# Sums of weight quarters in a Strassen-like FFN: added by transfers into the buffer instead of by VectorE

## The chip, the core and the metric

The kernel runs on one core of a Trainium2 chip. The metric is the device time of one execution in microseconds, taken without the profiler; the kernel before has a median of 1122.21 us over 3 runs (1121.78 to 1122.27). The engines of the core are TensorE (PE; its weight loads are listed as PEld), VectorE (DVE), ScalarE (ACT), GpSimd (POOL) and SyncE (SP). SP and POOL issue transfers here; 16 DMA queues carry them.

## What is computed

A bidirectional encoder block on 512 tokens of width 1024, in float32: FFN 1, a mixer (a recurrent branch and a neighbourhood attention), FFN 2. Only the two FFNs matter here:

```python
D_MODEL = 1024; SEQ = 512; D_FF = 2816; FFN_RES = 0.5

def _swiglu(h, w_gu, w_down):
    g, u = jnp.split(h @ w_gu, 2, axis=-1)
    return (jax.nn.silu(g) * u) @ w_down

x = x + FFN_RES * _swiglu(_rmsnorm(x, norm_ffn1[l]), w_ffn1_gu[l], w_ffn1_down[l])
...
x = x + FFN_RES * _swiglu(_rmsnorm(x, norm_ffn2[l]), w_ffn2_gu[l], w_ffn2_down[l])
```

## The kernel before

Tokens lie along the free dimension, features along the 128 partitions. To get float32 accuracy out of a faster format, each operand is split in two halves, H (a rounded copy, made by ScalarE, L138) and L (what is left, made by VectorE, L141), and each product takes three matmuls: H with H, H with L, L with H. Such a split of a 128x1024 block of weights is what `operand` does; its results lie in the pools wh and wl, four buffers each.

The hidden dimension has 22 blocks of 128 features. In FFN 1 the first 4 of them, in FFN 2 the first 2, are computed plainly from chunks of w1gu and w2gu. The others go two at a time through `strassen`: 9 units in FFN 1, 10 in FFN 2. A unit computes g and u of two blocks for all tokens. Its weights, as a 2 by 2 matrix (rows: g and u; columns: the two halves of the 1024 inputs) are four quarters of 128x1024 (512 KB) in w1s or w2s, numbered 0 to 3; the tokens are two halves of 256. Instead of eight products of a quarter with a half it makes seven, four of them with sums of quarters and of input tiles (Strassen's method in Winograd's form). Each product is 24 matmuls of 128x128 by 256 tokens and named by its input: a11 takes quarter 0, a12 quarter 2, s4 quarter 3, s1 the sum 0+1, s2 0+1+3, s3 1+3, and a22 0+1+3+2.

Per unit the buffers are a_ (quarter 0, then its running sum), b_ (quarter 3, then 3+1), d (quarter 1) and c (quarter 2). a_ and b_ come from the pool wraw (3 buffers, `load_w` also loads the plain and down-projection weights there), d and c from the pool pair (4 buffers). SP loads all four (L322). The sums are VectorE instructions (L325), each between two splits of the same buffer, run by the helper `after_sum` ahead of their turn (`high_priority`). The last product, a22, of a unit is made in the next unit, between s1 and s2, so TensorE's order within a unit is a11, a12, s1, a22 of the unit before, s2, s4, s3. In the last unit of an FFN, a12 moves behind s3. Results leave PSUM through p1, p5 and u2 (ScalarE L342, L348, L353; VectorE L337, L355, L357), are multiplied by rstd (L303), go through silu (L304) and are multiplied with u (L310).

A scheduler turns the program into one queue per engine, in which instructions run in order, each behind its semaphore waits. Instructions in `high_priority` are moved ahead.

Of the kernel before, what the change touches and what calls it, by code (L numbers as in the profile page):

```python
# [11 lines left out]
AF = mybir.ActivationFunctionType  # L12
ALU = mybir.AluOpType
# [71 lines left out]
def block_kernel(ctx: ExitStack, tc, a, out):  # L85
    nc = tc.nc
# [14 lines left out]
    def nm(s):  # L101
        uid[0] += 1
        return f"{s}_{uid[0]}"
# [3 lines left out]
    def big_t(dt=F32, shape=(P, T), n="b"):  # L107
        return big.tile(list(shape), dt, tag="big", bufs=NBIG, name=nm(n))

    def pair_t():  # L110
        return big.tile([P, 2, T], F32, tag="pair", bufs=4, name=nm("pair"))

    def acc_t():
        return acc.tile([P, T], F32, tag="acc", name=nm("acc"))

    def aux_t():
        return aux.tile([P, T], F32, tag="aux", name=nm("aux"))
# [18 lines left out]
    def split(raw, H, L, act=True):  # L136
        if act:
            nc.scalar.activation(H, raw, AF.Copy)  # L138
        else:
            nc.vector.tensor_copy(H, raw)  # L140
        nc.vector.tensor_tensor(L, raw, H.bitcast(F32), ALU.subtract)  # L141
# [3 lines left out]
    def raw_t():  # L145
        return wpool.tile([P, 1024], F32, tag="wraw", bufs=3, name=nm("wraw"))

    def hl_t():
        return (wpool.tile([P, 1024], F32R, tag="wh", bufs=4, name=nm("wh")),
                wpool.tile([P, 1024], F32R, tag="wl", bufs=4, name=nm("wl")))  # L150
# [124 lines left out]
    def strassen(src, units, A, r, hs, ahead):  # L275

        half = T // 2
        prev = {}
        view = lambda t: t.rearrange("p (m t) -> p m t", m=2)

        def product(ps, w, form, first, last):
            H, L = w
            for m in range(2):
                o = ps[:, m * half : (m + 1) * half]
                for k in range(4):
                    c = slice((m * 4 + k) * P, (m * 4 + k + 1) * P)
                    xh_, xl_ = A[form][k]


                    for w_, x_ in ((H, xh_), (H, xl_), (L, xh_)):  # L290
                        nc.tensor.matmul(o, w_[:, c], x_, start=first and m + k == 0 and w_ is H and x_ is xh_,  # L291
                                         stop=m + k == 4 and w_ is L, skip_group_check=True)

        def operand(raw):
            w = hl_t()
            with tc.high_priority():
                split(raw, *w)
            return w

        def gate(t, tok):  # L300
            rr = r[:, tok].unsqueeze(1).to_broadcast([P, 2, half])
            s_ = big_t(n="s")
            nc.vector.tensor_tensor(view(s_), view(t), rr, ALU.mult)  # L303
            nc.scalar.activation(s_, s_, AF.Silu)  # L304
            return s_

        def put(u, s_, t, tok):
            for m in range(2):
                c = slice(m * half, (m + 1) * half)
                mark["h"] = nc.vector.tensor_tensor(hs[u * 2 + m][:, tok], s_[:, c], t[:, c], ALU.mult)  # L310

        def last_product(p):
            product(p["Z"], p["w"](), "a22", False, True)
            put(p["u"], gate(p["Z"], slice(half, T)), p["u7"], slice(half, T))

        for u in range(units):
            a_, b_ = raw_t(), raw_t()
            d = pair_t().rearrange("p a b -> p (a b)")
            c = pair_t().rearrange("p a b -> p (a b)")

            for t, i in ((a_, 0), (d, 1), (b_, 3), (c, 2)):
                nc.sync.dma_start(t, src[u, i])  # L322

            def add(t, o, i):
                nc.vector.tensor_tensor(t, t, o, ALU.add)  # L325
            def after_sum(t, o, i, add=add):
                with tc.high_priority():
                    add(t, o, i)
                return operand(t)

            Z, X, Y = acc_t(), acc_t(), aux_t()
            hs += [big_t(n="h") for _ in range(2)]
            last = u == units - 1

            def gate1():
                product(Y, w_c, "a12", True, True)
                nc.vector.tensor_tensor(p1, p1, Y, ALU.add)  # L337
                return gate(p1, slice(0, half))

            product(Z, operand(a_), "a11", True, False)  # L340
            p1 = big_t(n="p1")
            nc.scalar.activation(p1, Z, AF.Copy)  # L342
            w_c = operand(c)
            if not last:
                s1 = gate1()
            product(X, after_sum(a_, d, 1), "s1", True, False)
            p5 = big_t(n="p5")
            nc.scalar.activation(p5, X, AF.Copy)  # L348
            if prev:
                last_product(prev)  # L350
            product(Z, after_sum(a_, b_, 3), "s2", False, False)
            u2 = big_t(n="u2")
            nc.scalar.activation(u2, Z, AF.Copy)  # L353
            product(X, operand(b_), "s4", False, True)
            nc.vector.tensor_tensor(u2, u2, X, ALU.add)  # L355
            product(Z, after_sum(b_, d, 1), "s3", False, False)
            nc.vector.tensor_tensor(p5, p5, Z, ALU.add)  # L357
            if last:
                ahead()
                s1 = gate1()  # L360
            put(len(hs) // 2 - 1, s1, u2, slice(0, half))
            prev = dict(u=len(hs) // 2 - 1, Z=Z, u7=p5, w=lambda a_=a_, c=c, f=after_sum: f(a_, c, 2))
        last_product(prev)

    def ffn(wgu, ws, wd, xh, xl, S, ssum, plain, res, emit_out, lead=None, end=None):
# [74 lines left out]
        def ahead(n):  # L440
            while len(cuts) < min(n, len(order)):
                qk = order[len(cuts)]
                cuts[qk] = big_t(F32R, n="hh"), big_t(F32R, n="hl")
                split(hs[qk[1]], *cuts[qk])

        strassen(ws, (FT - plain) // 2, A, r, hs, lambda: ahead(AHEAD))
        for q in range(2):
            outs = range(q * 4, q * 4 + 4)
# [517 lines left out]
    for w, fn, scale in ((0, AF.Gelu_apprx_tanh, 1.0), (1, AF.Tanh, 0.5)):  # L966
        for fs in (range(0, 4), range(4, 8)):
            for f, t in gates(w, fs, fn, scale):
                until("lru", lambda: A[f] is not None)
                if w == 0:  # L970
                    o = big_t(n="A")
# [118 lines left out]
```

## Time and profile before

| | |
|---|---|
| median of 3 runs | 1122.21 us |
| profiled execution, own time | 1122.16 us |
| its span (first to last instruction) | 1119.9 us |
| PE granted clock | 1.0 throughout |
| units of FFN 1 and FFN 2 | 9 and 10, of 20.16 us each |
| product (24 matmuls) | 2.88 us |
| sums on VectorE (L325) | 76, of 1.22 us |
| transfers | 138.04 MB, mean 123 GB/s |

The profile is one execution recorded by the hardware. A line such as "L141 DVE TENSOR_TENSOR wl<-wraw,wh" names the line of the kernel, the engine, the operation and its output and inputs by their tiles, with buffer numbers left out. In a timeline the columns are start (us), duration (us), engine, line, operation, and in brackets the idle time of the engine just before and what ended it. SPq and POOL rows with DMA are the issue of a transfer; the time to its landing is listed apart.

### The profile page before, as it was taken

How to read it: one execution, taken by the hardware profiler on the slowest of the kernel's cores; microseconds unless marked ns; L12 is line 12 of the kernel's file. 1: busy time of each engine (PE TensorE's matmuls, PEld its weight loads, DVE VectorE, ACT ScalarE, POOL GpSimd, SP SyncE). 2: the span in 40 equal slices, each digit the busy share in tenths (PEclk: the TensorE clock that was granted, in tenths of full speed). 3: DMA queues.
4: the chain of work that ended last, by engine and by line, in shares of the span. 5: the costliest groups of instructions: out<-in, count | busy, mean ns of one | idle time of the engine just before them, and what ended most of it. 6: DMA issues, size and time to landing. Idle time of an engine off the chain costs nothing.

```text
span 1119.9 us, 17423 instructions
## 1 busy us (share of the span) xinstructions
PE 1113.1 (99%) x6867; PEld 983.9 (88%) x6867; DVE 835.1 (75%) x1294; ACT 593.0 (53%) x897; POOL 52.4 (5%) x116
## 2 busy tenths in 40 slices
PE   9999999999999999999999999999999999999998
PEld 8899999988888778787888888888999999998887
DVE  7888888894745776998655976659788888894552
ACT  8554554563533669876464564446445455464330
POOL 0000000000000341310110000000000000000000
PEclk9999999999999999999999999999999999999999
DMA  7232333343433585653443332264134233353421
GB/s 265 95 124 85 113 114 95 120 144 95 136 91 107 160 255 154 184 164 95 144 140 104 104 104 72 75 237 164 57 96 131 77 115 113 94 170 95 132 76 38
DMA packets 46770, 138.04 MB, mean 123 GB/s; under 512 B 7008, under 2 KB 10592, under 8 KB 46688
## 3 DMA queue, kind: packets, MB, share of 16 engines
q1 hardware_dynamic: 39744, 118.31, 33.9%
q0 software_dynamic: 6368, 18.36, 5.8%
q8 instruction: 54, 0.88, 0.3%
q10 hardware_dynamic: 576, 0.26, 0.1%
q14 instruction: 28, 0.23, 0.1%
HBM read 120.12 MB, written 8.39 MB: 115 GB/s over the span
## 4 chain that ended last, share of the span: by engine, by line
PE 99%; DVE 0%; ACT 0%; issue 0%; ACTq 0%; DVEq 0%
PE acc L291 29%; PE acc L165 11%; PE acc L166 11%; PE acc L167 11%; PE aux L291 5%; PE acc L763 4%; PE acc L765 4%; PE acc L764 4%; PE aux L165 4%; PE aux L166 4%; PE aux L167 4%; PE aux L898 1%; PE aux L886 1%; PE aux L677 1%; PE aux L857 1%; PE acc L404 1%
## 5 line engine op out<-in xcount | busy, mean ns | idle before, releaser
L138 ACT ACTIVATE wh<-wraw 128x1024 fp32r<-128x1024 f32 (+3 forms) x242 | 239.7, 993 | 304.3 <-PE acc L291 95.9
L141 DVE TENSOR_TENSOR wl<-wraw,wh 128x1024 fp32r<-128x1024 f32 (+3 forms) x254 | 289.1, 1143 | 135.7 <-ACT wh L138 134.7
L291 PE MATMUL acc<-s,wh 128*128 128x256 f32 x1216 | 220.5, 283 | 0.0
L291 PEld LDWEIGHTS acc<-s,wh 128*128 128x128 f32 x1216 | 189.7, 192 | 0.0
L291 PE MATMUL acc<-s,wl 128*128 128x256 f32 x608 | 172.1, 283 | 0.0
L165 PE MATMUL acc<-xh,wh 128*128 128x512 f32 x304 | 121.1, 399 | 0.0
L167 PE MATMUL acc<-xh,wl 128*128 128x512 f32 x304 | 119.0, 391 | 0.0
L166 PE MATMUL acc<-xl,wh 128*128 128x512 f32 x304 | 118.9, 391 | 0.0
L291 PEld LDWEIGHTS acc<-s,wl 128*128 128x128 f32 x608 | 116.7, 192 | 0.0
L291 PE MATMUL acc<-xh,wl 128*128 128x256 f32 x304 | 86.0, 283 | 0.0
L291 PE MATMUL acc<-xl,wh 128*128 128x256 f32 x304 | 86.0, 283 | 0.0
L291 PE MATMUL acc<-xh,wh 128*128 128x256 f32 x304 | 86.0, 283 | 0.0
L763 PE MATMUL acc<-wh,xh 128*128 128x512 f32 x192 | 75.6, 394 | 0.0
L765 PE MATMUL acc<-wl,xh 128*128 128x512 f32 x192 | 74.9, 390 | 0.0
L764 PE MATMUL acc<-wh,xl 128*128 128x512 f32 x192 | 74.9, 390 | 0.0
L325 DVE TENSOR_TENSOR wraw<-wraw,pair 128x1024 f32<-128x1024 f32 x57 | 69.6, 1220 | 0.8
L165 PE MATMUL aux<-hh,wh 128*128 128x512 f32 (+1 forms) x181 | 69.9, 386 | 0.0
L166 PE MATMUL aux<-hl,wh 128*128 128x512 f32 (+1 forms) x181 | 69.9, 386 | 0.0
L167 PE MATMUL aux<-hh,wl 128*128 128x512 f32 (+1 forms) x181 | 69.9, 386 | 0.0
L165 PEld LDWEIGHTS acc<-xh,wh 128*128 128x128 f32 x304 | 57.1, 188 | 12.8 <-issue 1.7
L167 PE MATMUL acc<-hh,wl 128*128 128x512 f32 (+1 forms) x176 | 67.9, 386 | 0.0
L166 PE MATMUL acc<-hl,wh 128*128 128x512 f32 (+1 forms) x176 | 67.9, 386 | 0.0
(212 smaller groups left out, 2215.6 us busy)
## 6 DMA issues: line engine op xcount, KB each, us to landing
wraw<-wqkv SPq DMA_DIRECT2D x24, 512.0 KB, 4.8
wraw<-wg SPq DMA_DIRECT2D x24, 512.0 KB, 3.6
wraw<-w1d SPq DMA_DIRECT2D x22, 512.0 KB, 3.6
wraw<-w2d SPq DMA_DIRECT2D x22, 512.0 KB, 3.6
pair<-w2s SPq DMA_DIRECT2D x20, 512.0 KB, 3.6
wraw<-w2s SPq DMA_DIRECT2D x20, 512.0 KB, 3.7
wraw<-w1s SPq DMA_DIRECT2D x18, 512.0 KB, 3.6
pair<-w1s SPq DMA_DIRECT2D x18, 512.0 KB, 3.6
```

Of the source, the lines that this page charges most:

```text
L138: nc.scalar.activation(H, raw, AF.Copy)
L141: nc.vector.tensor_tensor(L, raw, H.bitcast(F32), ALU.subtract)
L165: nc.tensor.matmul(ps, wh, xh, start=first, stop=False, skip_group_check=skip)
L166: nc.tensor.matmul(ps, wh, xl, start=False, stop=False, skip_group_check=skip)
L167: mark["mm"] = nc.tensor.matmul(ps, wl, xh, start=False, stop=last, skip_group_check=skip)
L291: nc.tensor.matmul(o, w_[:, c], x_, start=first and m + k == 0 and w_ is H and x_ is xh_, stop=m + k == 4 and w_ is L, skip_group_check=True)
L325: nc.vector.tensor_tensor(t, t, o, ALU.add)
L404: nc.tensor.matmul(pre[i], w[i][1][:, s], xh[k], start=k == 0, stop=False)
L677: prev, mm = mm, nc.tensor.matmul(ps[d][b], W[w][o, c], X[x][o], start=x == 1, stop=w + x == 0)
L763: nc.tensor.matmul(pss[j], xh[kk][:, tj], H[:, s], start=kk == 0, stop=False)
L764: nc.tensor.matmul(pss[j], xl[kk][:, tj], H[:, s], start=False, stop=False)
L765: mark["mm"] = nc.tensor.matmul(pss[j], xh[kk][:, tj], L[:, s], start=False, stop=kk == KT - 1)
```

## The change

The sums move from VectorE to the transfers: a quarter is loaded by a GpSimd transfer that adds what it brings to what is in the buffer (`accum_op=ALU.add`). There are four such per unit: quarters 1, 3 and 2 into a_, one after the other, each behind the split of the sum before it, and quarter 3 into d, which holds quarter 1; s3 then reads d. b_ and c are only read. The 76 VectorE sums are gone. Each unit now moves eight quarters instead of four, four by SP and four by GpSimd. The load of a_, its product a11 and the copy into p1 stand in a function `begin`, called at the head of a unit (`begun` stays empty).

```diff
+        def begin(u):
+            a_ = raw_t()
+            nc.sync.dma_start(a_, src[u, 0])
+            Z = acc_t()
+            product(Z, operand(a_), "a11", True, False)
+            p1 = big_t(n="p1")
+            nc.scalar.activation(p1, Z, AF.Copy)
+            return a_, Z, p1
+
+        def add(u, t, i):
+            with tc.high_priority():
+                nc.gpsimd.dma_start(t, src[u, i], accum_op=ALU.add)
+
+        begun = {}
         for u in range(units):
-            a_, b_ = raw_t(), raw_t()
+            a_, Z, p1 = begun.pop(u) if u in begun else begin(u)
+            b_ = raw_t()
             d = pair_t().rearrange("p a b -> p (a b)")
             c = pair_t().rearrange("p a b -> p (a b)")
-            for t, i in ((a_, 0), (d, 1), (b_, 3), (c, 2)):
+            add(u, a_, 1)
+            for t, i in ((c, 2), (d, 1), (b_, 3)):
                 nc.sync.dma_start(t, src[u, i])
-            def add(t, o, i):
-                nc.vector.tensor_tensor(t, t, o, ALU.add)
-            def after_sum(t, o, i, add=add):
-                with tc.high_priority():
-                    add(t, o, i)
-                return operand(t)
+            add(u, d, 3)
...
-            product(X, after_sum(a_, d, 1), "s1", True, False)
+            w = operand(a_)
+            add(u, a_, 3)
+            product(X, w, "s1", True, False)
...
-            product(Z, after_sum(a_, b_, 3), "s2", False, False)
+            w = operand(a_)
+            add(u, a_, 2)
+            product(Z, w, "s2", False, False)
...
-            product(Z, after_sum(b_, d, 1), "s3", False, False)
+            product(Z, operand(d), "s3", False, False)
...
-            prev = dict(u=len(hs) // 2 - 1, Z=Z, u7=p5, w=lambda a_=a_, c=c, f=after_sum: f(a_, c, 2))
+            prev = dict(u=len(hs) // 2 - 1, Z=Z, u7=p5, w=lambda a_=a_: operand(a_))
```

How the queues change is shown on one unit in the middle of FFN 1 (the fifth). First VectorE before, from the split of s1 to the split of the next unit's a11; wraw_1502 is a_, wraw_1503 b_, pair_1504 d, pair_1505 c, wraw_1270 and wraw_1734 are a_ of the units before and after.

```order
L141 TENSOR_TENSOR wl_1579<-wraw_1502,wh_1578 128x1024
L325 TENSOR_TENSOR wraw_1502<-wraw_1502,wraw_1503 128x1024
...
L141 TENSOR_TENSOR wl_1610<-wraw_1270,wh_1609 128x1024
L141 TENSOR_TENSOR wl_1644<-wraw_1502,wh_1643 128x1024
L325 TENSOR_TENSOR wraw_1502<-wraw_1502,pair_1505 128x1024
L337 TENSOR_TENSOR p_258_1543<-p_258_1543,aux_1512 128x512
L141 TENSOR_TENSOR wl_1674<-wraw_1503,wh_1673 128x1024
L303 TENSOR_TENSOR s_1574<-p_258_1543,rstd_470 128x512
L325 TENSOR_TENSOR wraw_1503<-wraw_1503,pair_1504 128x1024
L141 TENSOR_TENSOR wl_1704<-wraw_1503,wh_1703 128x1024
L303 TENSOR_TENSOR s_1637<-acc_1278,rstd_470 128x512
L141 TENSOR_TENSOR wl_1748<-wraw_1734,wh_1747 128x1024
```

The same place of VectorE in the changed kernel; here wraw_1503 is a_, wraw_1536 b_, pair_1537 d, and wraw_1271 and wraw_1735 are a_ of the units before and after.

```order
L141 TENSOR_TENSOR wl_1581<-wraw_1503,wh_1580 128x1024
...
L368 TENSOR_TENSOR p_236_1377<-p_236_1377,acc_1273 128x512
L141 TENSOR_TENSOR wl_1612<-wraw_1271,wh_1611 128x1024
L141 TENSOR_TENSOR wl_1645<-wraw_1503,wh_1644 128x1024
L347 TENSOR_TENSOR p_251_1534<-p_251_1534,aux_1545 128x512
L303 TENSOR_TENSOR s_1577<-p_251_1534,rstd_470 128x512
L141 TENSOR_TENSOR wl_1676<-wraw_1536,wh_1675 128x1024
L141 TENSOR_TENSOR wl_1705<-pair_1537,wh_1704 128x1024
L303 TENSOR_TENSOR s_1639<-acc_1273,rstd_470 128x512
L141 TENSOR_TENSOR wl_1739<-wraw_1735,wh_1738 128x1024
```

The sums are gone, and the splits keep their order: s1, a22 of the unit before, s2, s4, s3, a11 of the next unit. ScalarE in the changed kernel, from the split of s1 to the split of the next a11:

```order
L138 ACTIVATE wh_1580<-wraw_1503 128x1024
L138 ACTIVATE wh_1611<-wraw_1271 128x1024
L323 ACTIVATE p_251_1534<-acc_1505 128x512
L138 ACTIVATE wh_1644<-wraw_1503 128x1024
L138 ACTIVATE wh_1675<-wraw_1536 128x1024
L304 ACTIVATE s_1577<-s_1577 128x512
L138 ACTIVATE wh_1704<-pair_1537 128x1024
L357 ACTIVATE p_264_1609<-acc_1544 128x512
L138 ACTIVATE wh_1738<-wraw_1735 128x1024
```

Its order stays as it was. GpSimd's queue, empty in the FFNs before, now has four adding transfers per unit; shown with their waits for this unit and the first of the next (pair_1769 is the next unit's d; DMASW and DMAHW are landings of transfers of POOL and SP, DVE the last split).

```order
L328 DMA wraw_1503<-w1s 128x1024 [waits DMAHW6_49,DMASW4_49,DVE_49]
L328 DMA pair_1769<-w1s 128x1024 [waits DMAHW0_49,DMASW2_49]
L328 DMA wraw_1503<-w1s 128x1024 [waits DMASW1_49,DVE_49]
L328 DMA wraw_1503<-w1s 128x1024 [waits DMASW3_49,DVE_49]
L328 DMA wraw_1735<-w1s 128x1024 [waits DMAHW2_49,DMASW0_49,DVE_49]
```

Each add into a_ waits for VectorE's half of the split before it, and the next unit's d has its add between the first and the second of a_.

More of the change, by code (lines that the diff above doesn't have):

```diff
@@ L314, in last_product @@
             put(p["u"], gate(p["Z"], slice(half, T)), p["u7"], slice(half, T))
+        def begin(u):
[10 more added lines that the diff above has]
+        begun = {}
         for u in range(units):
-            a_, b_ = raw_t(), raw_t()
+            a_, Z, p1 = begun.pop(u) if u in begun else begin(u)
+            b_ = raw_t()
             d = pair_t().rearrange("p a b -> p (a b)")
             c = pair_t().rearrange("p a b -> p (a b)")
-            for t, i in ((a_, 0), (d, 1), (b_, 3), (c, 2)):
+            add(u, a_, 1)
+            for t, i in ((c, 2), (d, 1), (b_, 3)):
                 nc.sync.dma_start(t, src[u, i])
-            def add(t, o, i):
-                nc.vector.tensor_tensor(t, t, o, ALU.add)
-            def after_sum(t, o, i, add=add):
-                with tc.high_priority():
-                    add(t, o, i)
-                return operand(t)
-            Z, X, Y = acc_t(), acc_t(), aux_t()
+            add(u, d, 3)
+            X, Y = acc_t(), aux_t()
             hs += [big_t(n="h") for _ in range(2)]
@@ L338, in gate1 @@
                 return gate(p1, slice(0, half))
-            product(Z, operand(a_), "a11", True, False)
-            p1 = big_t(n="p1")
-            nc.scalar.activation(p1, Z, AF.Copy)
             w_c = operand(c)
```

## The prediction

> **What bounds the kernel now.** The first view is the page: the busy time of each engine and the chain that ended last, and the two groups of instructions that the change removes (the second of them from the list of groups with different shapes kept apart; columns: busy time, mean of one in ns, idle time before them).
>
> ```profile
> PE 1113.1 (99%) x6867; PEld 983.9 (88%) x6867; DVE 835.1 (75%) x1294; ACT 593.0 (53%) x897; POOL 52.4 (5%) x116
> PE 99%; DVE 0%; ACT 0%; issue 0%; ACTq 0%; DVEq 0%
> L325 DVE TENSOR_TENSOR wraw<-wraw,pair 128x1024 f32<-128x1024 f32 x57 | 69.6, 1220 | 0.8
> L325 DVE TENSOR_TENSOR wraw<-wraw,wraw 128x1024 f32<-128x1024 f32 x19 | 23.2, 1220 | 0.1
> ```
>
> TensorE is busy for 1113.1 of 1119.9 us and alone makes up the chain. The 76 sums (57 + 19, so 92.8 us of VectorE) are on no path that sets the end. What a faster VectorE could give back is the idle time of TensorE, 6.8 us in all. The windows show where: the FFN 1 stage, then one unit of it (columns: window, its length, busy time and count of each engine, granted clock, DMA share, GB/s).
>
> ```profile
> 60.00:240.00 180.00, 179.10 (x1465) 177.72 (x1465) 155.81 (x192) 95.96 (x118) 0.00 (x0) 1.00 0.37 115
> 149.67:169.83 20.16, 20.16 (x171) 20.16 (x170) 17.27 (x22) 10.14 (x12) 0.00 (x0) 1.00 0.34 105
> ```
>
> In 180 us TensorE is idle for 0.9 us, and in one unit never, at full clock. So the change can win almost nothing; the question is whether it makes the weights late. The chain in order of time (start, us, what) gives the beat of a unit.
>
> ```profile
> 152.71 2.88 PE aux L291 x24
> 155.59 17.28 PE acc L291 x144
> 172.87 2.88 PE aux L291 x24
> ```
>
> The aux rows are the product a12 of two neighbouring units, 20.16 us apart; seven products of 2.88 us lie between, in the order a12, s1, a22 of the unit before, s2, s4, s3, a11. So here s1 starts at 155.59, s2 at 161.35, the next a11 at 169.99, and the next s2 at 181.51. The timelines of ScalarE and VectorE show the splits (H by L138, L by L141) that prepare them.
>
> ```profile
> 152.68 1.06 ACT L138 ACTIVATE wh<-wraw 128x1024 fp32r<-128x1024 f32 x1 [1.81 <-PE acc L291]
> 159.00 0.62 ACT L304 ACTIVATE s<-s 128x512 f32<-128x512 f32 x1
> 161.31 1.06 ACT L138 ACTIVATE wh<-wraw 128x1024 fp32r<-128x1024 f32 x1 [0.44 <-PE acc L291]
> 153.77 1.23 DVE L141 TENSOR_TENSOR wl<-wraw,wh 128x1024 fp32r<-128x1024 f32 x1 [1.23 <-ACT wh L138]
> 156.17 0.68 DVE L337 TENSOR_TENSOR p<-p,aux 128x512 f32<-128x512 f32 x1
> 156.77 1.22 DVE L141 TENSOR_TENSOR wl<-wraw,wh 128x1024 fp32r<-128x1024 f32 x1
> 162.05 0.69 DVE L303 TENSOR_TENSOR s<-acc,rstd 128x512 f32<-128x512 f32 x1
> 162.65 1.22 DVE L141 TENSOR_TENSOR wl<-wraw,wh 128x1024 fp32r<-128x1024 f32 x1
> ```
>
> The first ScalarE row is the split for s2: it starts at 152.68, its L is done at 153.77 + 1.23 = 155.0, and TensorE wants it at 161.35. A split is thus ready some 6 us ahead, and takes 155.0 - 152.68 = 2.3 us. It starts no earlier because it waits for TensorE to give back one of the four weight buffers ("<-PE acc L291"). The row at 161.31 is the split of the next a11; its L ends at 162.65 + 1.22 = 163.87, 6.1 us before 169.99.
>
> **What the change puts there.** Before, a sum is one VectorE instruction of 1.22 us, run early, between two splits. After, a sum is a transfer: it may start only when both halves of the last split have read the buffer, and the next split may start only when it has landed. Call X the time from the end of that L to the start of the next H. Within one unit three links then hang on each other: L of a11, X, split of s1, X, split of s2. From 163.87 the s2 split is done at 163.87 + 2X + 2 x 2.3, and 181.51 is when TensorE wants it. **That leaves 2X of 13.0 us, or 6.5 us each, once.**
>
> It also repeats. On both engines the splits run in program order, so when s2 is late, everything behind it is. By the rows of the changed order, behind H of s2 come: L of s2 (done 2.32 us after that H began), on VectorE the sum with Y and the multiplication by rstd (L337 and L303 here: the second starts 2.22 + 0.60 after, and lasts 0.69, so 3.5), on ScalarE the silu (0.62) and H of s3 (1.06), on VectorE its L (1.23), the multiplication for a22 (0.60 to the next start, 162.05 to 162.65) and L of the next a11 (1.22): 3.5 + 0.62 + 1.06 + 1.23 + 0.60 + 1.22 = 8.2 us. A unit therefore cannot be shorter than 2X + 2.3 (split of s1) + 8.2 = **2X + 10.5 us**, against 20.16 now. Below X = 4.8 nothing is lost; above, 2 us per unit and per us of X.
>
> **X.** No transfer of the trace adds, so X is bounded from both sides. POOL's plain transfers are the nearest rows, beside SP's (columns: count, size, median us to landing; then the least, median and longest of bm; then a VectorE row and the POOL issue that it released):
>
> ```profile
> wraw<-w1s SPq DMA_DIRECT2D x18, 512.0 KB, 3.6
> bm<-rpb POOLq DMA_DIRECT2D x16, 384.0 KB, 4.7
> DMA to landing us min/median/max: 3.2/4.7/8.3
> 567.38 0.08 DVE L869 DVE_READ_ACCUMULATOR2_ANT nmx<- 128x1 f32 x1
> 567.52 1.21 POOL L805 DMA_DIRECT2D bm<-rpb  x2 [0.63 <-DVE nmx L869]
> ```
>
> POOL issues 0.06 us after its releaser has ended (567.46 to 567.52); I take as much again, 0.1 rounded up, for ScalarE after the landing. Issue to landing is 4.7 us for 384 KB. Four transfers of 512 KB fill 0.34 of a unit, so one is 0.34 x 20.16 / 4 = 1.71 us of all 16 queues, and the missing 128 KB are 0.43. An adding transfer must fetch what the buffer holds as well as what comes: between nothing and another 1.71 us. Low end: 3.2 + 0.43 + 0.06 = 3.7. High end: landings in the crowded stretch below (7.2) + 0.43 + 1.71 + 0.16 = 9.5. I take the median row with the full second read, since both operands are 512 KB: 4.7 + 0.43 + 1.71 + 0.16 = **7.0 us**.
>
> The Trainium skill says more on the second read: "Collectives: The Full Stack", section "The bandwidth ceiling: the fold count and why AG ≠ RS ≠ AR", puts a transfer that adds at about half the rate of one that copies, since it reads two sources. It speaks against this change and agrees with the term of 1.71; no run here shows it yet. Without that term, X would be 5.3 and the sum below 15 us.
>
> **The sum, against the profiled execution's own 1122.16 us** (span 1119.9, 2.3 us lie around it; the median of the runs is 1122.21, so the two are taken as one).
> - Removed: 92.8 us of VectorE, worth 0, since TensorE never waits for them.
> - FFN 1 has 9 units, FFN 2 has 10. Unit 0 of each is free: it runs between plain chunks. The rows are
>
> ```profile
> 45.17 1.06 ACT L138 ACTIVATE wh<-wraw 128x1024 fp32r<-128x1024 f32 x1 [0.52 <-PE acc L166]
> 56.51 5.65 PE acc L291 x47
> ```
>
>  The split for its s1 starts at 45.17; 2.3 + 7.0 + 2.3 later, at 56.8, s2 is ready, and s2 starts some 2.9 us into the second row, at 59.4.
> - Unit 1 of each: 2X - 13.0 = 1.0, so 2.0.
> - Units 2 to 8 and 2 to 9, 15 in all: 2 x 7.0 + 10.5 - 20.16 = 4.34 each, 65.1.
> - The last unit of each leaves a12 for later, so s2 is wanted one product (2.88) earlier: 5.8.
>
> Total 72.9 us, or 34X - 165 in general; 1122.2 + 72.9 = **1195 us**. The other two adds hang on nothing near: POOL issues the add into the next unit's d between the two of a_ (the POOL rows above), a unit before s3 wants it, and the add for a22 has from s2 to a22, six products or 17 us, for X and a split. What stands behind a waiting split: on VectorE the sum of s3 into p5 (L357 here) waits with s1's split, and the product a22, which adds to the accumulator that it reads, waits for it; the product s1 lies between and covers 2.88 us of it. SP's queue keeps its order of loads; a_'s next buffer comes free at a22's split, as now:
>
> ```profile
> 142.00 10.90 SPq L322 DMA_DIRECT2D wraw<-w1s  x2
> ```
>
> The second of these two was issued at 142.00 + 10.90 - 0.33 = 152.6, 9 us ahead of the H at 161.31 that wants it, and lands in 3.6; that cover of 5 us stays.
>
> **The rivals.**
>
> *Not slower: the add lands like a plain transfer.* If the second read runs beside the first and the queues are quiet, X is 3.7 to 4.8, every link stays inside the cover of 6 us, and the time is 1122. For it: the fastest bm landed in 3.2 us, and the DMA share of a unit is only 0.34. Against it: the median is 4.7 for three quarters of the bytes. It decides at X = 4.8. The skill's "DMA: Bandwidth & Descriptors", section "Anatomy of one DMA — SWDGE (gpsimd) path", gives 2.0 us plus bytes over 436 GB/s, an estimate of 3.2 us for 512 KB. By that page the change would be free; the bm rows, 4.7 us for less, lie above it.
>
> *Much slower: the queues crowd.* The 4 loads of a unit are 6.9 us of queue time; 4 adds at 2 x 1.71 bring 13.7, in all 20.5 of 24.5 us, a share of 0.84. The trace has a stretch like that:
>
> ```profile
> 374.00:427.00 53.00, 53.00 (x256) 41.23 (x255) 37.65 (x50) 36.87 (x57) 27.65 (x60) 1.00 0.89 247
> bm<-rpb POOLq DMA_DIRECT2D x4, 384.0 KB, 7.2
> wraw<-wqkv SPq DMA_DIRECT2D x8, 512.0 KB, 7.7
> ```
>
> At a share of 0.89 landings took 7.2 and 7.7 us. X would be 9.5 at the most, and the time 1122 + 34 x 9.4 - 165 = 1277. Against it: a longer unit thins the traffic out again, and the median of 4.7 already holds some crowded rows.
>
> *Faster*: TensorE's 6.8 idle us are at the edges of stages; 1120 at best.
>
> **How the numbers follow.** Chances: X between 4.9 and 8 (1124 to 1230, the forecast) 0.63; X above 8 (the crowd) 0.22; X below 4.9 (no loss) 0.13; faster 0.02. The range takes in the no-loss end and X up to 9.4: 1122 to 1277. A measurement of this kernel tells a difference of about 0.2%, 2.2 us, from none; so faster 0.02, same 0.13, slower 0.85.
>
> **What would show it.** Right: a12 starts of neighbouring units about 24.5 us apart instead of 20.16, all of the gap in front of s2 (3 to 4 us) and s1; "ACT wh <- DMA wraw" as a new wait, 38 times or so; VectorE 93 us lighter; adds of 6.5 to 7 us to landing; no change outside the FFNs. Wrong: gaps in front of a11, b's or d's products (then a load or POOL's order is late, not the chain of adds); units of 20.16 us (X below 4.8); or landings over 9 us with a DMA share near 1 (then the queues are the bound).

## The result, and the profile after

The changed kernel takes 1191.34 us (median of 4 runs, 1184.14 to 1193.43) against 1122.24 us before (1121.78 to 1122.28) on the same chip: 1.0605 times as long, with an interval of 1.0589 to 1.0621. The forecast was 1195. The profiled execution took 1193.43 us itself.

The page first: its span, the busy engines, POOL's DMA queue (packets, MB, share of 16 engines), and the chain that ended last.

```profile
span 1191.7 us, 17520 instructions
...
PE 1139.3 (96%) x6867; PEld 997.4 (84%) x6867; DVE 747.7 (63%) x1218; ACT 583.5 (49%) x897; POOL 117.5 (10%) x192
...
q0 software_dynamic: 17312, 58.21, 25.3%
...
PE 62%; DMA 9%; DVE 4%; ACT 3%; issue 3%; ACTq 0%; DVEq 0%
```

VectorE is 87 us lighter (835.1 before); both groups of sums are gone from the list. (Their rows add up to 92.8 us, but neighbouring rows of a full queue overlap a little: 156.17 + 0.68 and 156.77 in the prediction's view.) TensorE no longer makes up the chain alone: transfers have 9% of the span in it, and splits and evictions a few more. The view follows the chain back only to 230 us, so most of FFN 1 is not in it. The same stages in windows (columns as in the prediction):

```profile
60.00:280.00 220.00, 196.99 (x1496) 188.96 (x1495) 124.35 (x171) 95.54 (x125) 26.57 (x31) 0.98 0.71 171
790.00:1050.00 260.00, 239.23 (x1742) 225.69 (x1741) 145.38 (x193) 112.12 (x145) 33.61 (x40) 0.98 0.72 171
```

TensorE, idle for 0.9 of 180 us in FFN 1 before, now idles 23 of 220 us there and 21 of 260 in FFN 2, and the DMA share has nearly doubled, from 0.37 to 0.71. The table of waits says who waits for whom (us in total, times, longest):

```profile
ACT wh L138 <- DMA wraw<-w2s: 103.3, 18, 7.7
ACT wh L138 <- DMA wraw<-w1s: 98.1, 17, 7.5
...
PE acc L291 <- DVE wl L141: 14.6, 20, 0.8
PE acc L291 <- ACT wh L138: 14.0, 13, 3.0
PE acc L291 <- ACT u L364: 11.4, 14, 4.7
PE acc L291 <- ACT p L357: 6.3, 12, 0.5
```

ScalarE's splits wait 35 times, 201 us in all, for an adding transfer. TensorE then waits for those splits, and also for two evictions (L357, L364) that stand behind them on ScalarE.

One unit in full, from the timelines of ScalarE, VectorE and POOL in FFN 2:

```profile
977.15 2.01 ACT L138 ACTIVATE wh<-wraw 128x1024 fp32r<-128x1024 f32 x2 [6.16 <-DMA wraw<-w2s]
...
991.29 2.01 ACT L138 ACTIVATE wh<-wraw 128x1024 fp32r<-128x1024 f32 x2 [4.92 <-DMA wraw<-w2s]
...
1000.42 2.00 ACT L138 ACTIVATE wh<-wraw 128x1024 fp32r<-128x1024 f32 x2 [6.65 <-DMA wraw<-w2s]
...
984.18 1.22 DVE L141 TENSOR_TENSOR wl<-wraw,wh 128x1024 fp32r<-128x1024 f32 x1
...
992.38 1.23 DVE L141 TENSOR_TENSOR wl<-wraw,wh 128x1024 fp32r<-128x1024 f32 x1 [4.12 <-ACT wh L138]
...
985.76 0.86 POOL L328 DMA_DIRECT2D wraw<-w2s  x1 [4.94 <-DVE wl L141]
...
993.96 0.85 POOL L328 DMA_DIRECT2D wraw<-w2s  x1 [4.20 <-DVE h L310]
```

H of s2 starts at 977.15 (the row holds two splits, s2 and s4). The L of the next a11 ends at 984.18 + 1.22 = 985.40: a tail of 8.25 us, against 8.2 in the prediction. POOL issues the first add at 985.76, and H of s1 starts at 991.29, so X is 5.89. Its L ends at 993.61, POOL issues at 993.96, and the next H of s2 starts at 1000.42: X is 6.81. Together 8.25 + 5.89 + 2.32 + 6.81 = 23.27, and 1000.42 - 977.15 = 23.27. Nothing else is in the loop.

The transfers (count, size, median us to landing), and below them, from the answer for the line of the adds, what POOL needs to issue one (least, median and longest ns, first and last start):

```profile
wraw<-w2s POOLq DMA_DIRECT2D x30, 512.0 KB, 5.7
...
wraw<-w1s SPq DMA_DIRECT2D x18, 512.0 KB, 5.2
...
pair<-w2s POOLq DMA_DIRECT2D x10, 512.0 KB, 7.6
```

```profile
L328 POOL DMA_DIRECT2D wraw<-w1s x27: 847/857/1007, 30.2 to 246.9; - x27
```

An add into a_ lands in 5.7 us; the plain loads beside it have gone from 3.6 to 5.2.

The last unit of FFN 1 is worse than the others (POOL's timeline and ScalarE's, then TensorE's waits between 235 and 270):

```profile
246.92 0.85 POOL L328 DMA_DIRECT2D wraw<-w1s  x1 [7.21 <-DVE wl L141]
...
255.33 1.06 ACT L138 ACTIVATE wh<-wraw 128x1024 fp32r<-128x1024 f32 x1 [6.50 <-DMA wraw<-w1s]
256.29 0.58 ACT L364 ACTIVATE u<-acc 128x512 f32<-128x512 f32 x1
```

```profile
PE acc L291 <- ACT u L364: 4.7, 1, 4.7
```

The third add (for a22) is issued at 246.92, its split starts at 255.33, and the copy u stands behind that split on ScalarE. The product s3, which adds onto the accumulator that u copies, waits 4.7 us for it.

### The profile page after: what moved, and what is told of

It reads as the page before. It is cut to its first block, busy times and chain, and to the rows that moved or that the text cites. A ratio compares the mean times of both kernels' runs of the same rounds, so it can differ in the third digit from the quotient of the medians.

```text
span 1191.7 us, 17520 instructions
## 1 busy us (share of the span) xinstructions
PE 1139.3 (96%) x6867; PEld 997.4 (84%) x6867; DVE 747.7 (63%) x1218; ACT 583.5 (49%) x897; POOL 117.5 (10%) x192
## 3 DMA queue, kind: packets, MB, share of 16 engines
q0 software_dynamic: 17312, 58.21, 25.3%
## 4 chain that ended last, share of the span: by engine, by line
PE 62%; DMA 9%; DVE 4%; ACT 3%; issue 3%; ACTq 0%; DVEq 0%
PE acc L165 10%; PE acc L167 10%; PE acc L166 10%; DMA wraw<-w2s 7%; PE acc L291 4%; PE acc L774 4%; PE acc L775 4%; PE acc L776 4%; PE aux L165 3%; PE aux L167 3%; PE aux L166 3%; ACT wh L138 3%; DVE wl L141 2%; DMA wraw<-w1s 2%; PE aux L909 1%
## 5 line engine op out<-in xcount | busy, mean ns | idle before, releaser
L141 DVE TENSOR_TENSOR wl<-wraw,wh 128x1024 fp32r<-128x1024 f32 (+3 forms) x235 | 265.7, 1136 | 287.3 <-ACT wh L138 280.9
L138 ACT ACTIVATE wh<-wraw 128x1024 fp32r<-128x1024 f32 (+3 forms) x223 | 215.5, 983 | 396.2 <-DMA wraw<-w2s 103.3
L291 PE MATMUL acc<-s,wh 128*128 128x256 f32 x1216 | 235.8, 294 | 31.9 <-ACT wh L138 14.0
L291 PEld LDWEIGHTS acc<-s,wh 128*128 128x128 f32 x1216 | 196.8, 199 | 40.6 <-ACT wh L138 17.4
L291 PE MATMUL acc<-s,wl 128*128 128x256 f32 x608 | 178.7, 294 | 14.6 <-DVE wl L141 14.6
L291 PEld LDWEIGHTS acc<-s,wl 128*128 128x128 f32 x608 | 121.0, 199 | 18.8 <-DVE wl L141 18.8
L165 PE MATMUL acc<-hh,wh 128*128 128x512 f32 (+1 forms) x176 | 67.9, 386 | 0.0
```

Of the source, the lines that this page charges most:

```text
L165: nc.tensor.matmul(ps, wh, xh, start=first, stop=False, skip_group_check=skip)
```

## The experiments

The theory: one loop sets the unit, 2X + 10.5 us, with X from the end of an L to the next H. The rivals: the added traffic, whoever waits for it; the latency of each add by itself; late loads; TensorE at a reduced clock. All ratios are to the kernel before, on the same chip.

**e1, sums in a buffer of their own.** Edit (e is a new tile with two buffers):

```
-            add(u, a_, 1)
-            for t, i in ((c, 2), (d, 1), (b_, 3)):
+            for t, i in ((e, 1), (c, 2), (d, 1), (b_, 3)):
                 nc.sync.dma_start(t, src[u, i])
+            add(u, e, 0)
             add(u, d, 3)
...
-            w = operand(a_)
-            add(u, a_, 3)
+            w = operand(e)
+            add(u, e, 3)
```

> The sums for s1, s2 and a22 are made in a buffer of their own (e), which is loaded with quarter 1 and takes quarter 0 by an adding transfer as soon as it is there, far ahead; a_ holds quarter 0 for a11 alone. All four adds of a unit stay transfers, and one plain load of 512 KB comes on top, so there is more traffic than in the changed kernel; but L of a11 no longer stands ahead of the split for s1, and the chain of a unit holds one X, not two. Chain theory: a unit needs X + 10.5, some 17 us at X = 6.4, less than 20.16, so 1122 to 1128 us. Traffic rival (the loss comes from the bytes and the landings, wherever they stand): 1190 us or more. Between the two, with units of 21 to 23 us, both would have a part.

1185.03 us, ratio 1.0559 (1.0542 to 1.0576): against my theory as it stood. The timelines of POOL, ScalarE and VectorE show why.

```profile
141.19 0.87 POOL L331 DMA_DIRECT2D pair<-w1s  x1 [8.64 <-DMA pair<-w1s]
141.74 1.20 POOL L331 DMA_DIRECT2D wlong<-w1s  x1
...
153.08 1.06 ACT L138 ACTIVATE wh<-wlong 128x1024 fp32r<-128x1024 f32 x1 [8.15 <-DMA wlong<-w1s]
...
140.04 1.22 DVE L141 TENSOR_TENSOR wl<-wlong,wh 128x1024 fp32r<-128x1024 f32 x1
```

The loop does hold one X only, but that X is 153.08 - 141.26 = 11.8 us. The add into d, held back by its load, was issued 0.55 us ahead of the add for s2. By the trace the first of the two landed 5.6 us after its issue, as an add alone does, and the second after 11.3 us: the later one waited. With an X of 11.8, one is as dear as two of 6. So the edit took away one X and lengthened the other: it settles nothing between loop and traffic.

**e2, the traffic alone.** The kernel before, with four adds per unit into spare buffers:

```
+                if dum is not None:
+                    n = dummy[nd[0] % 2]
+                    nd[0] += 1
+                    after(nc.gpsimd.dma_start(n, src[dum[0], dum[1]], accum_op=ALU.add), l, True)
```

> The kernel before, with all its sums on VectorE, and four adding transfers per unit more, released by the ends of the same splits, but into two spare buffers that nobody reads. Same bytes as the changed kernel, no split waits for them. Chain theory: 1122 to 1126 us, with the loads of SP slowed to 5 us or so. Traffic rival: 1150 to 1190 us, with waits of ScalarE for plain loads.

1121.55 us, ratio 0.9996 (0.9986 to 1.0005). The window of FFN 1:

```profile
60.00:220.00 160.00, 159.10 (x1326) 158.89 (x1325) 137.33 (x158) 80.85 (x97) 27.37 (x32) 1.00 0.92 209
```

With the DMA share at 0.92, higher than in the changed kernel, TensorE is idle 0.9 of 160 us. Plain loads landed in 4.5 to 5.9 us, and nobody was late for it. Here the bytes alone cost nothing.

**e3, the sum for s1 alone; e4, those for s1 and s2.** e4 takes the other two sums back to VectorE, e3 also that for s2:

```
-            add(u, d, 3)
...
-            add(u, a_, 2)
...
-            product(Z, operand(d), "s3", False, False)
+            product(Z, after_sum(b_, d), "s3", False, False)
...
+            prev = dict(u=len(hs) // 2 - 1, Z=Z, u7=p5, w=lambda a_=a_, c=c, f=after_sum: f(a_, c))
```

> Only the sum for s1 is an adding transfer; those for s2, s3 and a22 are back on VectorE. One X between two splits per unit. Chain theory: a unit needs X + 1.2 (the sum for s2) + 10.5, some 17.5 us, so nothing is lost: 1122 to 1126 us, though ScalarE's split for s1 waits for its transfer. Rival (each add costs what it lands beyond the cover of some 6 us, on its own): about a quarter of the loss, 1139 us.

> The sums for s1 and s2 are adding transfers; those for s3 and a22 are back on VectorE. Two X per unit, at half of the added bytes. Chain theory: the steady unit is 2X + 10.5 with the X that the trace shows; at 5.7 to 6.4 units of 21.9 to 23.3 us, and 1150 to 1178 us in all; with s1 alone free, the two together cost far more than twice one. Traffic rival: half of the loss, and no link between X and the unit: 1157 us. That the third add makes the end of each FFN dear shows here as an end that costs 5 to 8 us less.

e3: 1145.17 us, ratio 1.0205 (1.0190 to 1.0220); e4: 1215.18 us, ratio 1.0830 (1.0812 to 1.0848). Both are above what I expected of them, and e4, with half of the adds, is slower than the change with all four. The timeline of VectorE in e3, from the L of one a11 to that of the next:

```profile
148.44 1.21 DVE L141 TENSOR_TENSOR wl<-wraw,wh 128x1024 fp32r<-128x1024 f32 x1
...
157.77 1.22 DVE L342 TENSOR_TENSOR wraw<-wraw,wraw 128x1024 f32<-128x1024 f32 x1
...
161.90 1.23 DVE L342 TENSOR_TENSOR wraw<-wraw,pair 128x1024 f32<-128x1024 f32 x1
...
165.38 1.22 DVE L342 TENSOR_TENSOR wraw<-wraw,pair 128x1024 f32<-128x1024 f32 x1
...
169.52 1.22 DVE L141 TENSOR_TENSOR wl<-wraw,wh 128x1024 fp32r<-128x1024 f32 x1
```

All three sums stand inside the loop: they are behind the split that waits, and ahead of the L that the next add waits for. My expectation had counted the first and left out those for s3 and a22. The two L's end at 149.65 and 170.74, 21.1 us apart, of which X is 5.8; so the rest is 15.3, where the change has 10.5 beside its two X. Three sums are 3.7 us of the 4.8 between them; the other 1.1 are not accounted for row by row. By its time alone e3 is nearer to the rival's 1139 us than to the 1122 to 1126 of my theory; it is the rows that speak for the loop, and e4. POOL's adds for s2, s1 and s2 again in e4:

```profile
127.01 0.88 POOL L328 DMA_DIRECT2D wraw<-w1s  x1 [9.27 <-DVE wl L141]
143.24 0.87 POOL L328 DMA_DIRECT2D wraw<-w1s  x1 [15.35 <-DVE wl L141]
153.38 0.86 POOL L328 DMA_DIRECT2D wraw<-w1s  x1 [9.26 <-DVE wl L141]
```

This unit takes 26.4 us; the six steady units of FFN 1 take 26.0 on average, against 23.8 in the change. The two X of a unit add up to 13.2 us in both kernels. What is left beside them is 12.8 us in each of the six, against 10.6: the two sums in the loop, 2.4 us, are about what it is longer by. VectorE's sums, worth nothing while TensorE was the bound, cost nearly their full length once VectorE's queue is part of the loop.

**e5, another order.** The same four adds; the split and first add of the next a11 come ahead of the split for s2, and the add into d is written behind the add of s2 (four buffers for a_ and b_):

```
+            nxt = None if last else begin(u + 1)
             w = operand(a_)
             add(u, a_, 2)
             product(Z, w, "s2", False, False)
...
+            if nxt:
+                begun[u + 1] = first(u + 1, *nxt)
```

> All four sums of a unit stay adding transfers into the same buffers with the same bytes; only the order changes. The split of the next unit's a11 and the add behind it are issued ahead of the split for s2, its product between s2 and s4, the add into d behind the second add of a_, and a_ and b_ have four buffers instead of three. A waiting split for s2 then no longer stands ahead of the L that lets the next unit's first add start: a loop holds one X, split of s1 2.3 + X + about 7 us of ScalarE's own splits to the next s1, some 16 us at X = 6.4, below 20.16. Queue-order theory: 1122 to 1130 us. If adds of this latency, or their traffic, cost the time however they are ordered: 1180 us or more.

**e6, the control for its buffers** (`bufs=3` to `bufs=4`).

> The changed kernel with four buffers instead of three for a_ and b_, nothing else: the control for the order experiment. The loop of two X is untouched, so the theory expects 1180 to 1195 us; loads that start sooner may shorten or lengthen X by some tenths (3.4 us for each tenth). If late loads had a part in the loss, 1150 us or less.

e6: 1190.75 us, ratio 1.0605 (1.0574 to 1.0636), as the changed kernel: loads were not late for want of a buffer. e5: 1153.13 us, ratio 1.0276 (1.0241 to 1.0311), more than half of the loss gone, but not all. What was left shows on POOL, ScalarE and VectorE:

```profile
132.55 0.86 POOL L334 DMA_DIRECT2D pair<-w1s  x1 [8.01 <-DMA pair<-w1s]
133.26 1.03 POOL L334 DMA_DIRECT2D wraw<-w1s  x1
...
143.05 1.06 ACT L138 ACTIVATE wh<-wraw 128x1024 fp32r<-128x1024 f32 x1 [5.65 <-DMA wraw<-w1s]
...
131.68 1.23 DVE L141 TENSOR_TENSOR wl<-wraw,wh 128x1024 fp32r<-128x1024 f32 x1 [1.60 <-ACT wh L138]
```

It is e1's collision again. Though the edit writes it behind, the add into d stands ahead of the add for s2 in POOL's queue, here by 0.7 us, and X is 143.05 - 132.91 = 10.1.

**e9, that collision taken away.** On top of e5's edit, the loads of c and d go a unit ahead (five buffers), and d's add is tied behind the add for a22:

```
-            add(u, a_, 2)
+            i = add(u, a_, 2)
+            if not last:
+                after(add(u + 1, cd[u + 1][1], 3), i)
```

> The order experiment again, with the add into d moved out of the way: in e5 it was issued 0.7 us ahead of the second add of a_ (132.55 and 133.26), and from the end of that L to the next H it then took 10.1 us (132.91 to 143.05), so the loop of one X was 2.3 + 10.1 + 8.1 = 20.5 us and more. Now the loads of c and d are issued a unit ahead (five buffers instead of four for them), and POOL issues the add into the next unit's d right behind the add for a22, when no split waits. All four adds and their bytes stay. Queue-order theory: X back to 6.4 or 7, the loop 16.7 to 17.5 us, the time 1122 to 1132 us. If one X of this size in a unit is dear by itself, or the traffic is: 1150 us or more, as e5.

1128.51 us, ratio 1.0058 (1.0043 to 1.0073). One view each: the window of FFN 1, the timelines of POOL and ScalarE, the landing of d's adds, and the only wait of TensorE in the FFNs:

```profile
60.00:220.00 160.00, 160.00 (x1336) 160.00 (x1335) 103.99 (x124) 79.32 (x96) 25.82 (x30) 1.00 0.88 207
```

```profile
148.59 0.88 POOL L334 DMA_DIRECT2D wraw<-w1s  x1 [9.44 <-DVE wl L141]
...
154.56 1.06 ACT L138 ACTIVATE wh<-wraw 128x1024 fp32r<-128x1024 f32 x1 [1.82 <-PE aux L291]
```

```profile
pair<-w2s POOLq DMA_DIRECT2D x10, 512.0 KB, 10.0
```

```profile
PE acc L291 <- ACT u L381: 5.7, 2, 3.1
```

All four adds, a DMA share of 0.88, and TensorE is busy for 160.00 of 160.00 us. The split for s2 shown starts when TensorE returns a buffer ("<-PE aux"), as before the change, not when its add lands. In the seven units of FFN 1 between the first and the last it is so five times; once, at 175.84, the split waited for its add, and TensorE did not wait for the split. d's adds, issued last, land in 10 us, and nobody waits for them. The earlier loads and the new place of d's add were not tried one without the other. The rest, 5.7 of 6.6 us, is the wait for the copy u in the two last units.

**e7, the second read.** POOL's transfers write instead of adding; the sums of the quarters are left out:

```
-                nc.gpsimd.dma_start(t, src[u, i], accum_op=ALU.add)
+                nc.gpsimd.dma_start(t, src[u, i])
```

> The changed kernel with POOL's transfers writing the buffer instead of adding to it, in the same places with the same waits; the sums of the quarters are left out, so s1, s2, a22 and s3 are multiplied by bare quarters. It measures the second read. By the prediction's term (1.71 us of 7.0 for the second read) X falls from 6.4 to about 4.7, the loop 2X + 10.5 to 20.16, and the time to 1122 to 1130 us. If issue and latency make X and the second read nothing, 1180 to 1191 us; in between, 34 us for each us of X.

1121.40 us, ratio 0.9999 (0.9990 to 1.0009). The whole loss is gone with the same waits in the same places. One view each: landings, POOL's queue, and the window of FFN 1:

```profile
wraw<-w2s POOLq DMA_DIRECT2D x30, 512.0 KB, 3.9
```

```profile
q0 software_dynamic: 17312, 58.21, 17.3%
```

```profile
60.00:220.00 160.00, 160.00 (x1336) 160.00 (x1335) 101.96 (x125) 78.33 (x96) 16.39 (x31) 1.00 0.66 203
```

A transfer lands in 3.9 us instead of 5.7. POOL's queue took 17.3% of 1119.1 = 194 us instead of 25.3% of 1191.7 = 302; without the 65 us that the kernel before spends there (5.8% of 1119.9) and by 76 transfers, that is 1.69 us of all 16 engines for a plain one and 3.11 for an adding one, 1.84 times as much.

The Trainium skill ("Collectives: The Full Stack", "The bandwidth ceiling: the fold count and why AG ≠ RS ≠ AR") explains the half rate of a ReduceScatter, which adds, by the second source that it reads, and gives a measured ratio of 1.93 to an AllGather, which copies. The local transfers here, with 1.84, agree. The Trainium skill's fit for POOL's transfers ("DMA: Bandwidth & Descriptors", "Anatomy of one DMA — SWDGE (gpsimd) path"), 3.2 us by estimate for 512 KB, is below both rows, 3.9 and 5.7; the measurement decides.

**e8, filler for TensorE.** 16 more matmuls per unit in front of s1:

```
+            for k in range(4):
+                for t_ in range(4):
+                    x_ = A["s1"][k][t_ % 2]
+                    nc.tensor.matmul(X[:, :half], x_[:, :P], x_, start=True, stop=True, skip_group_check=True)
             product(X, w, "s1", True, False)
```

> The changed kernel with 16 more matmuls of 128 x 256 in each unit, in front of the product s1, on operands that are long there; they write the accumulator that s1 clears. They are 16 x 0.12 = 1.9 us of TensorE per unit, 36 us in 19 units. Chain theory: the unit is set by splits and adds, TensorE idles 3 to 4 us in it, so the filler costs nearly nothing, 0 to 8 us (1184 to 1199 us), most of it in the first and last units; the idle gaps get shorter and the granted clock rises. If TensorE at its reduced clock were the bound of the longer units: 1191 + 36 = 1227 us.

1199.46 us, ratio 1.0686 (1.0670 to 1.0702), 8 us above the changed kernel and just past the upper edge of the expectation. The steady units are no longer (23.66 us against 23.76, table below): there the work of the filler fits into TensorE's gaps. From H of s2 in unit 0 to that in unit 1 it takes 30.89 us instead of 25.54 in FFN 1 and 30.17 instead of 25.32 in FFN 2; there the filler did cost. The granted clock over the whole run was 0.993 instead of 0.990.

**e10 and e12, X made longer.** A fill of an unused tile on POOL between the L and the add for s1 and for s2 (640, then 1408 elements wide); the add into d is tied behind the add for s1:

```
+                if i in (1, 3) and not plain_d:
+                    m = nc.gpsimd.memset(junk, 0.0)
+                    after(m, mark["l"], True)
+                x = nc.gpsimd.dma_start(t, src[u, i], accum_op=ALU.add)
+                if m is not None:
+                    after(x, m)
+                    mark["add"] = x
+                elif plain_d:
+                    after(x, mark["add"])
```

> The changed kernel with a fill of an unused tile (128 x 640, GpSimd) between the L and the add for s1 and s2, so that only X grows, by the duration m of that fill and what it takes to issue, which the trace shows (my guess is 0.5 to 0.8 us). Chain theory: 2 us per unit for each us, 34 in all: 1191 + 34 x m, some 1208 to 1218 us. If the loop were closed by something else than X (loads, POOL's own queue, TensorE), less than 10 us more: below 1201.

> As e10, with a fill of 128 x 1408. In e10 the fill of 640 took 0.63 us but moved the issue of an add only from 0.35 to 0.70 us after its L, and X stayed at about 6.3 since the transfers landed sooner (the add into d there always stands behind the add for s1). By 0.63 us for 640, a fill of 1408 is about 1.4 us, so the issue comes some 1.46 us after the L, 0.76 later than in e10, with the same order on POOL. Chain theory: X about 7.0 to 7.1, a steady unit 0.76 x 2 = 1.5 us longer (24.4 to 24.7 against 22.9 to 23.1), 34 x 0.76 = 26 us on e10's 1192: 1208 to 1226 us. If X does not set the unit: 1185 to 1200 us, as e10.

e10: 1192.12 us (1184.35 to 1201.76), ratio 1.0654 (1.0605 to 1.0703): no longer than the change, so a miss. The add was issued only 0.35 us later, and X stayed near 6.4, since the transfers landed sooner. e12: 1247.91 us, ratio 1.1129 (1.1114 to 1.1145), more than expected. POOL's fill and add, and the H behind them:

```profile
207.24 1.28 POOL L331 MEMSET junk<- 128x1408 f32 x1 [6.38 <-DVE wl L141]
208.46 0.86 POOL L333 DMA_DIRECT2D wraw<-w1s  x1
...
215.77 2.00 ACT L138 ACTIVATE wh<-wraw 128x1024 fp32r<-128x1024 f32 x2 [8.16 <-DMA wraw<-w1s]
```

The L ended at 207.12 (205.89 + 1.23), so X is 8.65. The issue came 1.34 us after the L, about as planned, but from there to the H it took 7.3 us, where e10's adds landed in 5.6. So both sizes were missed. One thing differs in step with the adds for s2: SP's next load into the pool wraw is issued 1.74 us behind such an add in the changed kernel, 1.06 in e10 and 0.42 in e12, in nearly every unit. That it makes e12's adds land late is likely, but no run tests it alone. The law that the two runs test held, as the six steady units of FFN 1 show in each kernel (means; a unit runs from H of s2 to H of s2, all read from ScalarE's and VectorE's rows as in the unit above):

| kernel | unit | X for s1 | X for s2 | unit less both X |
|---|---|---|---|---|
| changed | 23.76 | 6.74 | 6.45 | 10.57 |
| e6 | 23.39 | 6.62 | 6.20 | 10.56 |
| e8 | 23.66 | 6.30 | 6.80 | 10.56 |
| e10 | 23.14 | 6.52 | 6.29 | 10.33 |
| e12 | 26.64 | 8.09 | 8.83 | 9.72 |
| e7 | 20.40 | 4.88 | 4.53 | 10.99 |

In the changed kernel the single units run from 22.59 to 25.16 us, and the last column is 10.55 to 10.57 in every one of them. (In e10 and e12 VectorE's order differs by a place or two, which shortens the tail. e7 lies where the two bounds meet: the first three of its units hold slack, 11.4 us in the last column, and the other three are at 10.56 again, with TensorE never waiting for a split.)

**e11, the last unit.** The sum for a22 back on VectorE in the last unit of each FFN:

```
-            add(u, a_, 2)
+            if not last:
+                add(u, a_, 2)
...
```

> The changed kernel with the sum for a22 back on VectorE in the last unit of each FFN; all else as it is. The prediction put 7.8 us on the first and last units of the two FFNs; the trace of the changed kernel has some 14 to 16 there. If the wait of the last a22's split for its add makes the difference (it stands ahead of the copy u on ScalarE, and the product s3 waits for that copy), 6 to 10 us go: 1181 to 1186 us. If the last units are late for other reasons, 1189 to 1193.

1179.75 us, ratio 1.0519 (1.0490 to 1.0548): 11.6 us less than the change, a little more than expected. TensorE's waits for u (L369 here) were 11.4 us before the edit, and are now these:

```profile
PE acc L291 <- ACT u L369: 4.1, 12, 0.3
```

The two long ones are gone; that is 7.3 of the 11.6 us. TensorE's own rows say the same: against the kernel before, the stretch from the start of the last s2 to the end of an FFN is longer by 7.3 us (FFN 1) and 5.1 us (FFN 2) in the change, and by 2.4 and 1.1 in e11, so 8.9 us are gained there. The rest is not accounted for one by one; runs of these kernels differ by that much among themselves.

## Why the prediction was right, and where it was off

- **TensorE was the bound, and 92.8 us of VectorE were worth nothing there:** right. e7 has no sums on VectorE either and takes as long as the kernel before, and e2 shows the old kernel's cover swallowing the traffic too.
- **The loop 2X + 10.5:** right to 0.1 us (10.6 in every steady unit; tail 8.25 for 8.2). It is shown by more than agreement: the same adds in another order (e9) give 1128.51, shorter transfers in the same order (e7) 1121.40, and the traffic without the waits (e2) 1121.55.
- **X of 7.0:** a little too long. In FFN 1 it is 6.6, the mean of 6.74 and 6.45. The second read was about right: 1.71 predicted, 1.8 by the landings of e7 (5.7 less 3.9), though 1.42 by queue time (3.11 less 1.69). The plain part was too long (4.7 + 0.43 predicted, 3.9 in e7), probably since the bm rows hold the crowded stretch that the prediction shows; the handoff was too short (0.16, where POOL alone takes 0.35 after an L).
- **The threshold at X = 4.8:** shown from one side by e7, whose mean X is 4.7 and in which TensorE never waits for a split. No kernel here with two X in its loop has a mean X between that and 6.3, so the exact place is only the sum's.
- **15 steady units, 65.1 us:** too much by 9.5. The adds for s2 in FFN 1 run from 74.08 to 238.85 in 7 units, in FFN 2 from 848.53 to 1041.78 in 8: 23.54 and 24.16 us each, so 7 x 3.38 + 8 x 4.00 = 55.6, the term being 2X with X too long.
- **First and last units, 7.8 us:** this step was too small. TensorE's last product of the FFNs moved by 33.7 and a further 38.0 us, 71.7 in all, so some 16 us lie in these units. (Counted by the starts of s2 on TensorE instead, the steady units have 59.3, and the stretch behind the last s2 of each FFN has 12.4, where the sum had 5.8.) The failed sentence is that the add for a22 "has from s2 to a22, six products or 17 us". In the last unit no next unit lies between, and its split stands ahead of the copy u; e11 takes it away and gains 11.6 us, 8.9 of them there. Too much in the one term and too little in the other nearly cancel, so that the total comes out this close is in part luck: 72.9 predicted, 71.3 in the profiled execution (1193.43 - 1122.16) and 69.1 between the medians (1191.34 - 1122.24).
- **The rival "lands like a plain transfer":** its condition was right and its premise false. A plain landing would have been free (e7), but an adding one takes 5.7 us, not 3.9.
- **The rival "queues crowd":** as a bound of its own it is refuted: at shares of 0.92 (e2) and 0.88 (e9) TensorE does not wait in the steady units. As a cause of a longer X it is real: two adds issued within 0.7 us made X 10.1 and 11.8 (e5, e1). (Its sum takes X as 9.4 where the high end above it is 9.5; that is 3 us of the 1277.)
- **Not foreseen:** the evictions behind the late splits (L357 and L364, 17.7 us of TensorE's waits), and the clock. Why X is 5.5 to 6.2 us in some units of the changed kernel's FFN 1 and 7.0 to 7.7 in others stays open; e10 and e12 moved it by as much without being made to.

## What to carry to other kernels

Before work is moved off an engine that nobody waits for, write down what the new way makes wait, and follow every in-order queue behind that wait until it comes back to its start: the sum of that loop, not the load of any engine, is the new bound. A transfer that adds in place to a buffer just read puts its whole latency into that loop; here two of them, 6.6 us each, beat a cover of 4.8. If such adds are wanted, order them so that a loop holds only one, and let the ones that nobody needs soon be issued last (e9: the same adds for 6.6 us instead of 69).

## What the hardware showed unasked

An adding transfer of 512 KB takes 3.11 us of all 16 DMA engines and a plain one 1.69; POOL needs 0.86 us to issue it, against 0.53 (e7). And TensorE's granted clock falls behind the gaps. Three windows of the changed kernel:

```profile
170.00:180.00 10.00, 6.97 (x49) 6.57 (x47) 3.65 (x4) 3.41 (x4) 0.86 (x1) 0.89 0.58 117
174.44:177.85 3.41, 1.06 (x6) 0.86 (x7) 1.82 (x2) 2.00 (x2) 0.26 (x1) 1.00 0.05 19
177.85:181.26 3.41, 3.41 (x18) 3.41 (x17) 2.88 (x3) 2.67 (x4) 0.60 (x1) 0.50 0.65 85
```

In the ten microseconds from 170 TensorE idles for 3.0 us, in two gaps, and the mean clock is 0.89. The other two windows show how: in the 3.41 us up to 177.85 TensorE works for 1.06, and for the next 3.41 us it has a clock of 0.50. In e12, whose gaps are up to 4.1 us, the whole run has 0.96. The Trainium skill ("TensorE: Matmul & The Clock Gate", "What's actually happening") says that the array falls to half clock after an idle window of about 3.4 us. The half clock and the 3.4 us agree with the rows; but neither of the two gaps was that long (the longer is 2.3 us), so 1.06 us of work in such a window did not keep the clock up.

TensorE's busy time rose by 26 us (1113.1 to 1139.3) for the same 6867 matmul rows. A mean clock of 0.990 over 1191.7 us accounts for some 12 of them at most; the rest is not explained here. Most of it cost no time, since the loop, not TensorE, set the unit (e8).
